# State space products first in each dense block, and the low halves of the dense weights on VectorE

## The chip, the cores and the metric

The kernel runs on one core of a Trainium2 chip. The metric is the time of one execution on the device in microseconds (us). The kernel before takes 3360.59 us, the median of three runs (3353.09 to 3363.12).

## What is computed

A decoder block over 2048 tokens of width 1024: a normalized input is projected to a state space branch (width 512), an attention branch (8 heads of 64, with an indexer that keeps 256 keys for each query) and two sets of gates. The branches are projected back to 1024 columns, gated, added, projected by w_out and added to the input; then follows a gated feed-forward layer (FFN) of width 2816.

```python
h = _rms(x, norm1_g[l])
proj = h @ w_in[l]
u, q, k, v, qi, ki, wi, gates = jnp.split(proj, IN_SPLITS, axis=-1)
y_ssm = _s5_branch(u, ...)
...
y_att = _dsa_branch(q, k, v, qi, ki, wi)
g_ssm, g_att = jnp.split(gates, N_BRANCH, axis=-1)
merged = (jax.nn.sigmoid(g_ssm) * (y_ssm @ w_proj_ssm[l])
          + jax.nn.sigmoid(g_att) * (y_att @ w_proj_attn[l]))
x = x + merged @ w_out[l]
h2 = _rms(x, norm2_g[l])
x = x + (jax.nn.silu(h2 @ w_ffn_gate[l]) * (h2 @ w_ffn_up[l])) @ w_ffn_down[l]
```

## The kernel before

**Precision.** Every large product is made of three matmuls: a float32 operand is split into a high part, rounded to fp32r, and a low part, the rest; high by high, high by low and low by high are summed in PSUM (mm3). Each weight has to be split once: a copy that rounds (hi) and a subtraction (lo).

**Stages.** The input projection, the state space scan and the gates come first. Then three generators run interleaved: state space, attention (for four groups of four tiles of 128 tokens: a search for each query's 256th score, called topk, then the attention of the four tiles), and dense. Dense works in four blocks of 512 tokens; block tb needs the attention of tiles 4tb to 4tb+3. A class (Pace) keeps an estimate of when each engine is free, while the program is recorded, and picks the generator that can go on first; this fixes each engine's order once and for all. At run time every engine goes through its own list in order and waits on semaphores. SP issues all DMAs, in order as well.

**A dense block** (block):
- *Products of the branches.* For each of the 8 column tiles ct (128 columns) and each branch br (0 state space, 1 attention) there are 12 matmuls of 128 x 512 into a PSUM bank f. VectorE multiplies the gate g by it. Gates are stored in DRAM; each branch has two buffers for them, and a buffer is loaded again when its last user is done. Before, the branches alternate after a first group of four, and every second product ends with a merge: the two gated products are added (on POOL or DVE), ScalarE rounds the sum into mg, and DVE or POOL subtracts for its low half.
- *Output projection.* 192 matmuls f<-ww,mg; x1 holds the input rows and the sum.
- *Norm and FFN.* Transposes, then gate and up products (f<-h,ww) and down products (f<-wd,at) added into x1, which is stored to out.

The generator waits before a block until the attention of its four tiles is done (attended). The state space half of a block's input (act, from act_d) and the attention half (act, from att_d) are loaded by load_branch.

**Weights** (Rings, a Loader). In block 0 each item, 512 KB, is loaded to raw (two buffers), split into ww (a ring of four) or wd, and the split pair is stored to DRAM (wc<-ww, 1 MB). Blocks 1 to 3 load the pair again (ww<-wc). Before, an item of the branch products holds one column tile of both branches. hi goes to POOL, DVE or ScalarE and lo to POOL or DVE, whichever the planner has free first (spare); with tight set, DVE is left out of the choice.

**PSUM.** A block has 3 banks in the pool fps, 8 when attention is done for all 16 tiles; during a topk it may borrow 4 more (lend). In the trace nearly every line is L206, since one helper records all operations; names of tiles tell them apart. raw, ww, wd are weights, g gates, mg the merged rows, f the dense PSUM banks; lg, P, pt, th, tl, po, ya belong to attention, and tr, un, cnt, jkd, jka to the search.

Of the kernel before, what the change touches and what calls it, by code (L numbers as in the profile page):

```python
# [12 lines left out]
F32 = mybir.dt.float32  # L13
# [12 lines left out]
KD = D // 128  # L26
# [220 lines left out]
class Loader:  # L247


    def __init__(self, b, pool, bufs, items):  # L250
        self.b, self.pool, self.bufs, self.todo = b, pool, bufs, deque(items)
        self.here, self.count, self.allowed = deque(), 0, 0
        self.fill()
# [8 lines left out]
    def split(self):  # L262
        raw, dest = self.here.popleft()
        self.count += 1
        hi, lo = dest()
        p = self.b.pace
        eng = p.spare(hi, ("POOL", "DVE", "ACT"))
        if eng is p.gpsimd:
            eng.tensor_tensor(hi, raw, self.b.zeros[:, :1].to_broadcast(list(raw.shape)), op=ALU.add)
        elif eng is p.scalar:  # L270
            eng.copy(hi, raw)
        else:
            eng.tensor_copy(hi, raw)
        p.spare(lo).tensor_tensor(lo, raw, hi.bitcast(F32), op=ALU.subtract)
        self.fill()
# [14 lines left out]
class Rings(Loader):  # L290

    def __init__(self, b, pool, bufs, items):
# [70 lines left out]
class Block:  # L366
# [1295 lines left out]
    def weights(self):  # L1662

        a = self.a
        items = []
        for ct in range(KD):
            items.append(("w", lambda raw, ct=ct: [
                (raw[:, i * 512:(i + 1) * 512].rearrange("p (k c) -> p k c", k=4),
                 a[w][0, :, ct * 128:(ct + 1) * 128].rearrange("(k p) c -> p k c", p=128))
                for i, w in enumerate(("w_proj_ssm", "w_proj_attn"))]))  # L1670
        for half in range(2):
# [22 lines left out]

    def block(self, tb, bigp, ld, nps, nd):

# [6 lines left out]
        with ExitStack() as st:  # L1703
            psp = self.pool(st, "fps", nps, PSUM)
            x1 = self.pool(st, "x1", 1).tile([128, nt, D], F32, name="x1")
# [26 lines left out]
            with ExitStack() as sm:  # L1732
                mp = self.pool(sm, "mg", 1)
                mg = mp.tile([128, 2, KD, n], F32R, name="mg")
                with ExitStack() as sp:
# [3 lines left out]
                    def load_gate(ct, br):  # L1739
                        if ct < KD:  # L1740
                            gates[ct, br] = gp.tile([128, n], F32, name=f"g{br}")
                            nc.sync.dma_start(gates[ct, br], self.gate_d[br * KD + ct][hf][:, h0:h0 + n])
# [3 lines left out]
                    act = self.act  # L1746
                    act += [self.load_branch(bigp, br, tb) for br in range(len(act), 2)]
                    self.act = []
                    load_gate(1, 0)
                    load_gate(0, 1)  # L1750
                    load_gate(1, 1)
                    for q, (ct, br) in enumerate([(0, 0), (1, 0), (0, 1), (1, 1)] +
                                                 [(ct, br) for ct in range(2, KD) for br in range(2)]):
                        w = ld.get("w", 1 if q == 1 else 0)
                        w = w.rearrange("p z a (b k c) -> p (z a) b k c", b=2, k=4)[:, :, br]
                        yield ready(w, act[br])
                        ps = bank()
                        for k in range(4):
                            self.mm3(ps, w[:, 0, k], w[:, 1, k], act[br][:, 0, k], act[br][:, 1, k], k == 0, k == 3)
                            ld.tick()  # L1760
                        x = gates[ct, br]
                        nc.vector.scalar_tensor_tensor(x, x, 1.0, ps, op0=ALU.add, op1=ALU.mult)
                        if br == 1:
                            ld.drop("w")
                            x0, x = gates.pop((ct, 0)), gates.pop((ct, 1))
                            spare(x0).tensor_tensor(x0, x0, x, op=ALU.add)
                            self.split(x0, mg[:, 0, ct], mg[:, 1, ct], nc.scalar, spare(x0))
                            load_gate(ct + 2, 0)
                            load_gate(ct + 2, 1)
                        if q == 3:  # L1770
                            self.pace.tight = False
                        if q in (4, 6, 8, 10):
                            t = q // 2 - 2
                            nc.sync.dma_start(x1[:, t], a["x"][0, t0 + t * 128:t0 + (t + 1) * 128])
                fn = self.pool(sm, "fn", 1)
# [85 lines left out]
            ap = self.pool(st, "fa", 5)  # L1861
            tp = self.pool(st, "ft", 2)
            ld.ring("d", self.pool(st, "fd", nd), nd, 2)

# [94 lines left out]
    def run(self):  # L1959
# [12 lines left out]
        def dense(st, gates):  # L1972
# [4 lines left out]
            with ExitStack() as st:  # L1977
# [8 lines left out]
                for tb in range(NB):  # L1986
                    if tb == 1:
                        first.close()
                    yield lambda: self.pace.at("PE") if self.attended >= 4 * (tb + 1) else ("PE", 1e9, None)
                    alone = self.attended == NT  # L1990
                    if alone:
                        self.pace.BIAS = 0.0
                    yield from self.block(tb, bigp, ld, *((8, 2) if alone else (3, 1)))

# [30 lines left out]
```

## Time and profile before

| what | us |
|---|---|
| median of three runs | 3360.59 |
| lowest and highest | 3353.09, 3363.12 |
| the profiled execution | 3357.88 |
| its span | 3355.8 |
| first branch product of block 0 | starts at 980.8 |
| first branch product of block 3 | starts at 2888.7 |

PE is TensorE, PEld its loading of weights, DVE VectorE, ACT ScalarE, POOL GpSimd, SP the queue that issues DMAs. "Busy" counts the time in which an instruction was running. In a timeline row stand the start, the length, engine, line, operation, output <- inputs, and in brackets how long the engine had been idle and what ended that. Matmuls overlap: a row gives some 0.39 us for a 128 x 512 matmul, while they follow each other much faster, so PE's pace is read from how many fit into a stretch.

### The profile page before, as it was taken

How to read it: one execution, taken by the hardware profiler on the slowest of the kernel's cores; microseconds unless marked ns; L12 is line 12 of the kernel's file. 1: busy time of each engine (PE TensorE's matmuls, PEld its weight loads, DVE VectorE, ACT ScalarE, POOL GpSimd, SP SyncE). 2: the span in 40 equal slices, each digit the busy share in tenths (PEclk: the TensorE clock that was granted, in tenths of full speed). 3: DMA queues.
4: the chain of work that ended last, by engine and by line, in shares of the span. 5: the costliest groups of instructions: out<-in, count | busy, mean ns of one | idle time of the engine just before them, and what ended most of it. 6: DMA issues, size and time to landing. Idle time of an engine off the chain costs nothing. (4 is left out here: it accounts for less than half of the span.)

```text
span 3355.8 us, 42712 instructions
## 1 busy us (share of the span) xinstructions
PE 3171.5 (95%) x15528; PEld 2651.1 (79%) x15528; DVE 2106.4 (63%) x4532; ACT 1275.1 (38%) x2211; POOL 638.1 (19%) x628
## 2 busy tenths in 40 slices
PE   7999989899977999989999999999999999999999
PEld 6988767678755788877778888877888888788887
DVE  6555685555587766688687775876886666422223
ACT  3231544445552444346322443665314444210000
POOL 4323676522223311234100000001000000000000
PEclk9999999999988999999999999999999999999999
DMA  5743333534447775656847324366555332755543
GB/s 184 227 122 109 121 89 108 164 120 142 129 166 268 283 257 196 237 182 225 332 187 262 109 93 166 140 236 242 197 213 182 119 108 88 268 195 219 207 177 149
DMA packets 312961, 605.56 MB, mean 180 GB/s; under 512 B 46352, under 2 KB 194608, under 8 KB 282032
## 3 DMA queue, kind: packets, MB, share of 16 engines
q1 hardware_dynamic: 312752, 602.85, 51.7%
q8 instruction: 122, 2.00, 0.2%
q14 instruction: 87, 0.71, 0.1%
HBM read 434.70 MB, written 166.89 MB: 179 GB/s over the span
## 5 line engine op out<-in xcount | busy, mean ns | idle before, releaser
L206 PE MATMUL f<-h,ww 128*128 128x512 f32 (+1 forms) x4416 | 1013.1, 384 | 1.3 <-DVE h L206 0.8
L206 PEld LDWEIGHTS f<-h,ww 128*128 128x128 f32 x4416 | 803.4, 191 | 156.5 <-DVE h L206 1.8
L206 PE MATMUL f<-wd,at 128*128 128x512 f32 x2112 | 518.2, 397 | 28.7 <-DVE t L206 6.5
L206 PEld LDWEIGHTS f<-wd,at 128*128 128x128 f32 x2112 | 396.3, 191 | 116.5 <-DVE t L206 8.1
L206 PE MATMUL gps<-hT,gw 128*128 128x512 f32 x1536 | 387.5, 403 | 4.6 <-ACT gsg L206 3.2
L206 ACT ACTIVATE jka<-S,tr 128x1920 bf16<-128x1920 f32 (+6 forms) x217 | 305.6, 1408 | 180.5 <-DVE tr L206 128.7
L206 PEld LDWEIGHTS gps<-hT,gw 128*128 128x128 f32 x1536 | 288.3, 193 | 68.5 <-ACT gsg L206 5.2
L206 PE MATMUL mm<-w,hT 128*128 128x512 f32 (+1 forms) x1152 | 282.8, 403 | 10.3 <-DVE hT L206 7.2
L206 DVE TENSOR_TENSOR x<-f,x 128x512 f32<-128x512 f32 x352 | 235.1, 686 | 77.0 <-PE f L206 76.4
L206 PEld LDWEIGHTS mm<-w,hT 128*128 128x128 f32 x1152 | 241.5, 239 | 36.7 <-DVE hT L206 8.6
L206 DVE TENSOR_TENSOR tl<-pt,th 128x512 fp32r<-128x512 f32 (+1 forms) x288 | 183.8, 658 | 120.9 <-ACT th L206 119.8
L206 DVE SCALAR_TENSOR_TENSOR t<-t,f 128x512 f32<-128x512 f32 (+1 forms) x123 | 82.1, 668 | 271.8 <-PE f L206 223.6
L206 ACT CAST th<-pt 128x512 fp32r<-128x512 f32 (+1 forms) x288 | 155.5, 563 | 223.8 <-PE pt L206 220.2
L206 PE MATMUL f<-act,ww 128*128 128x512 f32 x768 | 191.8, 411 | 29.5 <-POOL ww L206 20.4
L206 PEld LDWEIGHTS f<-act,ww 128*128 128x128 f32 x768 | 151.2, 199 | 69.5 <-POOL ww L206 24.2
L206 POOL TENSOR_TENSOR g<-g,g 128x512 f32<-128x512 f32 x31 | 39.8, 1285 | 793.9 <-DVE g L206 793.9
L206 PE MATMUL f<-ww,mg 128*128 128x512 f32 x768 | 180.3, 397 | 10.6 <-ACT ww L206 7.0
L206 ACT ACTIVATE P<-P,m 128x1024 f32<-128x1024 f32 (+7 forms) x192 | 172.3, 900 | 46.9 <-DVE m L206 46.8
L206 PE MATMUL lg<-kk,q 128*128 128x512 f32 (+1 forms) x640 | 183.3, 388 | 3.5 <-DMA kk<-kk 3.5
L206 ACT ACTIVATE t<-f 128x512 f32<-128x512 f32 (+1 forms) x92 | 52.9, 575 | 343.8 <-PE f L206 343.7
L206 PEld LDWEIGHTS f<-ww,mg 128*128 128x128 f32 x768 | 147.2, 192 | 43.2 <-ACT ww L206 7.9
L206 ACT CAST at<-t 128x512 fp32r<-128x512 f32 (+1 forms) x92 | 55.2, 600 | 325.4 <-DVE t L206 325.3
(361 smaller groups left out, 4497.9 us busy)
## 6 DMA issues: line engine op xcount, KB each, us to landing
ww<-wc SPq DMA_DIRECT2D x180, 1024.0 KB, 4.9
wd<-wc SPq DMA_DIRECT2D x66, 1024.0 KB, 7.2
wc<-ww SPq DMA_DIRECT2D x60, 1024.0 KB, 7.5
raw<-in_w_in_dram SPq DMA_DIRECT2D x104, 256.0 KB, 3.4
wc<-wd SPq DMA_DIRECT2D x22, 1024.0 KB, 6.3
x<-in_x_dram SPq DMA_DIRECT2D x32, 512.0 KB, 5.3
gate<-gsg SPq DMA_DIRECT2D x64, 256.0 KB, 2.2
g<-gate SPq DMA_DIRECT2D x64, 256.0 KB, 5.7
```

Of the source, the lines that this page charges most:

```text
L206: return f(*args, **kw)
```

## The change

Three things change.

- Items of the branch products hold two column tiles of one branch, state space first. A block makes its eight state space products first, keeps the gated results in x1 (which is free until the input rows are loaded, now after the merge of each pair), and then the eight attention products, each of which ends in a merge. The block starts when the attention of the *block before* is done, and the wait for its own stands between the two halves. The load of the attention half moves there too, or two products ahead of it if attention is done by then.
- The low halves of all dense weights are made by DVE, and the high halves by DVE or ACT, never by POOL. Since only block 0 splits weights, this concerns block 0.
- The pool fps always has 3 banks; when all attention is done, 5 more are lent.

```diff
+    ENGS = ("POOL", "DVE", "ACT")
...
-        eng = p.spare(hi, ("POOL", "DVE", "ACT"))
+        eng = p.spare(hi, self.ENGS)
...
-        p.spare(lo).tensor_tensor(lo, raw, hi.bitcast(F32), op=ALU.subtract)
+        low = p.spare(lo) if "POOL" in self.ENGS else p.vector
+        low.tensor_tensor(lo, raw, hi.bitcast(F32), op=ALU.subtract)
...
+    ENGS = ("DVE", "ACT")
...
-            psp = self.pool(st, "fps", nps, PSUM)
+            psp = self.pool(st, "fps", 3, PSUM)
...
-                    act += [self.load_branch(bigp, br, tb) for br in range(len(act), 2)]
+                    if not act:
+                        act.append(self.load_branch(bigp, 0, tb))
...
+                    kept = x1.rearrange("p t (a c) -> p (t a) c", a=2)
+                    for q in range(2 * KD):
+                        br, ct = q // KD, q % KD
+                        if q == KD:
+                            if self.attended < 4 * (tb + 1):
+                                yield lambda: at("PE") if self.attended >= 4 * (tb + 1) else ("PE", 1e9, None)
+                            if self.attended == NT:
+                                self.pace.BIAS = 0.0
+                                self.spare_banks = 5
+                        if q == KD - 2 or q == KD:
+                            if len(act) == 1 and self.attended >= 4 * (tb + 1):
+                                act.append(self.load_branch(bigp, 1, tb))
+                            if q < KD:
+                                load_gate(0, 1)
+                                load_gate(1, 1)
...
-                        x = gates[ct, br]
-                        nc.vector.scalar_tensor_tensor(x, x, 1.0, ps, op0=ALU.add, op1=ALU.mult)
-                        if br == 1:
+                        x = gates.pop((ct, br))
+                        if br == 0:
+                            nc.vector.scalar_tensor_tensor(kept[:, ct], x, 1.0, ps, op0=ALU.add, op1=ALU.mult)
+                        else:
+                            nc.vector.scalar_tensor_tensor(x, x, 1.0, ps, op0=ALU.add, op1=ALU.mult)
+                            spare(x).tensor_tensor(x, x, kept[:, ct], op=ALU.add)
+                            self.split(x, mg[:, 0, ct], mg[:, 1, ct], nc.scalar, spare(x))
+                        load_gate(ct + 2, br)
+                        if ct % 2 == 1:
                             ld.drop("w")
...
-                    yield lambda: self.pace.at("PE") if self.attended >= 4 * (tb + 1) else ("PE", 1e9, None)
...
+                    if self.attended < 4 * tb:
+                        yield lambda: self.pace.at("PE") if self.attended >= 4 * tb else ("PE", 1e9, None)
+                    yield from self.block(tb, bigp, ld)
```

**Where it moves instructions.** On POOL, at the start of block 0 (ww<-raw,zeros is a high half, ww<-raw,ww a low half, g<-g,g the sum of two gated products), there stands before:

```order
L206 TENSOR_TENSOR ww<-raw,zeros 128x1024
L206 TENSOR_TENSOR ww<-raw,ww 128x1024 x2
L206 TENSOR_TENSOR g_9373<-g_9373,g_9382 128x512
L206 TENSOR_TENSOR mg<-g_9373,mg 128x512
L206 TENSOR_TENSOR ww<-raw,ww 128x1024
L206 TENSOR_TENSOR g_9380<-g_9380,g_9384 128x512
```

In the change only the eight sums of each block are left there. The low halves stand on DVE, among the search's rows; the start of block 0 on DVE in the change:

```order
L206 SCALAR_TENSOR_TENSOR jkd,cnt_7815<-H_8577,tf_7816,jkd 128x320
L206 TENSOR_TENSOR ww<-raw,ww 128x1024
L206 TENSOR_SCALAR un_7812<-cnt_7808 128x1
L206 SCALAR_TENSOR_TENSOR tr_7811<-un_7812,tr_7811 128x1
L206 TENSOR_SCALAR jkd<-H_8577,tf_7816 128x320
```

The 53 low halves that POOL made are now DVE's, and the 24 high halves that POOL made are ACT's and DVE's.

On DVE in block 1, the gated products (g<-g,f before; x<-g,f for the kept ones in the change) and the low halves of the merged rows (mg<-g,mg). Before, from the fifth product on:

```order
L206 SCALAR_TENSOR_TENSOR g_14574<-g_14574,f 128x512
L206 SCALAR_TENSOR_TENSOR g_14576<-g_14576,f 128x512
L206 TENSOR_TENSOR mg<-g_14574,mg 128x512
L206 SCALAR_TENSOR_TENSOR g_14597<-g_14597,f 128x512
L206 SCALAR_TENSOR_TENSOR g_14599<-g_14599,f 128x512
L206 TENSOR_TENSOR mg<-g_14597,mg 128x512
```

And in the change, the last two of the state space half and, after a few rows of the search, the first of the attention half:

```order
L206 SCALAR_TENSOR_TENSOR x_14393<-g_14490,f 128x512
L206 SCALAR_TENSOR_TENSOR x_14393<-g_14506,f 128x512
L206 TENSOR_SCALAR un_13715<-cnt_13711 128x1
L206 SCALAR_TENSOR_TENSOR tr_13714<-un_13715,tr_13714 128x1
L206 TENSOR_SCALAR un_13724<-cnt_13720 128x1
L206 SCALAR_TENSOR_TENSOR tr_13723<-un_13724,tr_13723 128x1
L206 SCALAR_TENSOR_TENSOR g_14510<-g_14510,f 128x512
L206 TENSOR_TENSOR mg<-g_14510,mg 128x512
L206 SCALAR_TENSOR_TENSOR g_14512<-g_14512,f 128x512
L206 TENSOR_TENSOR mg<-g_14512,mg 128x512
```

Before, a merge follows every second product; now none follows the first eight and one follows each of the last eight.

On PE at the start of block 3 (act_24977 and act_24252 are the state space input, act_25469 and act_25605 attention's; po, pt and lg are attention). Before, the end of attention and the first products:

```order
L206 MATMUL f<-wd,at 128x512 x24
L206 MATMUL lg<-ident,s 8x128
L206 MATMUL lg<-r_25427,hsel 128x128 x8
L206 MATMUL f<-act_24977,ww 128x512 x24
L206 MATMUL f<-act_25469,ww 128x512 x24
```

In the change, first the start of the block, then the end of attention:

```order
L206 MATMUL f<-wd,at 128x512 x18
L206 MATMUL po<-th,v 128x256
L206 MATMUL po<-tl,v 128x256
L206 MATMUL f<-act_24252,ww 128x512 x12
L206 MATMUL pt<-ident,P 128x128 x8
L206 MATMUL f<-act_24252,ww 128x512 x12
L206 MATMUL lg<-kk,q 128x512 x4
```

```order
L206 MATMUL lg<-ident,s 8x128
L206 MATMUL lg<-r_25579,hsel 128x128 x8
L206 MATMUL f<-act_25605,ww 128x512 x96
L206 MATMUL f<-ww,mg 128x512 x192
```

Before, attention ended among block 2's last matmuls and two state space products stood between it and the first attention product. Now all eight state space products stand among attention's matmuls, and after the last of them come 48 matmuls lg<-kk,q, 128 transposes pt and 128 matmuls po with no dense matmul between them.

More of the change, by code (lines that the diff above doesn't have):

```diff
@@ L1665, in weights @@
         items = []
[L1666 to L1670, printed above, removed]
+        for w in ("w_proj_ssm", "w_proj_attn"):
+            for c0 in range(0, KD, 2):
+                items.append(("w", lambda raw, w=w, c0=c0: [
+                    (raw[:, i * 512:(i + 1) * 512].rearrange("p (k c) -> p k c", k=4),
+                     a[w][0, :, (c0 + i) * 128:(c0 + i + 1) * 128].rearrange("(k p) c -> p k c", p=128))
+                    for i in range(2)]))
         for half in range(2):
@@ L1693, in load_branch, with block @@
         return z
-    def block(self, tb, bigp, ld, nps, nd):
+    def block(self, tb, bigp, ld):
         nc, a, at = self.nc, self.a, self.pace.at
@@ L1746, in block @@
                     act = self.act
-                    act += [self.load_branch(bigp, br, tb) for br in range(len(act), 2)]
+                    if not act:
+                        act.append(self.load_branch(bigp, 0, tb))
                     self.act = []
                     load_gate(1, 0)
[L1750 to L1755, printed above, removed]
+                    kept = x1.rearrange("p t (a c) -> p (t a) c", a=2)
[13 more added lines that the diff above has]
+                                load_gate(1, 1)
+                        w = ld.get("w")
+                        w = w.rearrange("p z a (b k c) -> p (z a) b k c", b=2, k=4)[:, :, ct % 2]
                         yield ready(w, act[br])
@@ L1760, in block @@
                             ld.tick()
-                        x = gates[ct, br]
-                        nc.vector.scalar_tensor_tensor(x, x, 1.0, ps, op0=ALU.add, op1=ALU.mult)
-                        if br == 1:
-                            ld.drop("w")
[L1765 to L1769, printed above, removed]
+                        x = gates.pop((ct, br))
[7 more added lines that the diff above has]
+                        if ct % 2 == 1:
+                            ld.drop("w")
+                            if br == 1:
+                                t = ct // 2
+                                nc.sync.dma_start(x1[:, t], a["x"][0, t0 + t * 128:t0 + (t + 1) * 128])
                         if q == 3:
                             self.pace.tight = False
-                        if q in (4, 6, 8, 10):
-                            t = q // 2 - 2
-                            nc.sync.dma_start(x1[:, t], a["x"][0, t0 + t * 128:t0 + (t + 1) * 128])
                 fn = self.pool(sm, "fn", 1)
@@ L1862, in block @@
             tp = self.pool(st, "ft", 2)
+            nd = 2 if self.attended == NT else 1
             ld.ring("d", self.pool(st, "fd", nd), nd, 2)
@@ L1988, in dense @@
                         first.close()
-                    yield lambda: self.pace.at("PE") if self.attended >= 4 * (tb + 1) else ("PE", 1e9, None)
[L1990 to L1993, printed above, removed]
+                    if self.attended < 4 * tb:
+                        yield lambda: self.pace.at("PE") if self.attended >= 4 * tb else ("PE", 1e9, None)
+                    yield from self.block(tb, bigp, ld)
         st = ExitStack()
```

## The prediction

> **What bounds the kernel now.** The page comes first, then tables of stretches, then who waited for whom. The first line is the span; the profiled execution took 3357.88 us, so 2.1 us lie around it, and it stands 2.7 us below the median of the three runs shown, inside their spread of 10 us. All sums below are made against 3357.88. The second line gives busy time by engine.
>
> ```profile
> span 3355.8 us, 42712 instructions
> PE 3171.5 (95%) x15528; PEld 2651.1 (79%) x15528; DVE 2106.4 (63%) x4532; ACT 1275.1 (38%) x2211; POOL 638.1 (19%) x628
> ```
>
> PE is busy 95% of the span, so a gain must come out of stretches where PE waits or runs below its pace. The table of stretches gives that pace. Columns: the stretch, its length, busy time with count for PE, PEld, DVE, ACT, POOL, granted clock, DMA share, GB/s.
>
> ```profile
> 971.20:1111.40 140.20, 104.52 (x385) 79.70 (x385) 103.64 (x212) 36.95 (x53) 55.06 (x29) 0.87 0.80 277
> 1400.00:1620.00 220.00, 196.54 (x828) 157.94 (x828) 182.46 (x358) 119.83 (x152) 86.17 (x41) 0.95 0.64 229
> 1620.00:1664.00 44.00, 44.00 (x196) 36.44 (x195) 17.20 (x30) 7.50 (x11) 9.02 (x7) 1.00 0.94 361
> 2246.00:2290.00 44.00, 44.00 (x196) 36.44 (x195) 16.26 (x25) 4.52 (x9) 9.01 (x7) 1.00 0.93 349
> 2884.70:2904.30 19.60, 13.38 (x44) 9.36 (x42) 4.11 (x7) 0.62 (x1) 0.00 (x0) 0.83 0.68 226
> ```
>
> The third and fourth are the branch products of blocks 1 and 2: 196 matmuls in 44.00 us, 0.2245 us each, with nothing lost; but DMA is 0.93 to 0.94 busy there, which matters below. At that pace the 384 matmuls of block 0's products and output projection (first row) need 86.2 us and took 140.2: **54 us lost**. The second row, the end of block 0, has PE idle for 220 - 196.5 = **23.5 us**. The last is the start of block 3: 35 products (7.9 us) and some 1 us for attention's last matmuls in 19.6 us, 10.7 us lost.
>
> In the first stretch two engines end the waits:
>
> ```profile
> PE f L206 <- POOL ww L206: 23.9, 11, 9.5
> PE f L206 <- ACT ww L206: 11.8, 5, 4.6
> ```
>
> Both are the making of weights, 35.7 us. In the second stretch the timeline shows why DVE is late:
>
> ```profile
> 1485.20 2.35 POOL L206 TENSOR_TENSOR ww<-raw,zeros 128x1024 fp32r<-128x1024 f32 x1
> 1485.89 1.67 DVE L206 SCALAR_TENSOR_TENSOR tr<-un,tr 128x1 int32<-128x1 int32 x1
> 1487.62 2.40 POOL L206 TENSOR_TENSOR ww<-raw,ww 128x1024 fp32r<-128x1024 f32 x1
> 1487.66 2.38 DVE L206 SCALAR_TENSOR_TENSOR tr<-un,tr 128x1 int32<-128x1 int32 x1
> 1495.21 0.16 DVE L206 SCALAR_TENSOR_TENSOR tr<-un,tr 128x1 int32<-128x1 int32 x1
> 1497.67 2.92 PE L206 MATMUL f<-wd,at 128*128 128x512 f32 x6 [5.98 <-ACT t L206]
> ```
>
> An update of one number per partition takes 0.16 us alone and 2.38 us while POOL makes weights: DVE ends when POOL ends. PE then stood 5.98 us.
>
> **The change part by part.** First, who makes the weights of block 0:
>
> ```profile
> L206 POOL TENSOR_TENSOR ww<-raw,ww 128x1024 fp32r<-128x1024 f32 x43 | 106.3, 2472 | 153.5 <-ACT ww L206 146.0 <-DVE ww L206 6.3
> L206 POOL TENSOR_TENSOR wd<-raw,wd 128x1024 fp32r<-128x1024 f32 x10 | 25.5, 2550 | 127.0 <-ACT wd L206 126.7
> L206 ACT CAST ww<-raw 128x1024 fp32r<-128x1024 f32 x43 | 44.9, 1047 | 60.1 <-PE f L206 38.7 <-DMA raw<-in_w_out_dram 11.2 <-DMA raw<-in_w_ffn_up_dram 3.6
> L206 DVE TENSOR_TENSOR ww<-raw,ww 128x1024 fp32r<-128x1024 f32 x17 | 20.8, 1225 | 21.7 <-ACT ww L206 21.6
> ```
>
> 53 low parts go from POOL (2.47 to 2.55 us) to DVE (1.225 us): 53 x 1.225 = 65 us more on DVE. Against this stand up to 53 blocked DVE instructions, each of which lost up to 2.2 us; I take DVE's load as unchanged. Each weight is ready 2.47 - 1.225 = 1.25 us sooner.
>
> Stretch 971 to 1111: before, a weight's ACT cast stands behind the merge's cast, which waits for the product before it; with all state space products first, the casts of the attention weights stand ahead of the merges. The waits named above (35.7 us) can go, but 140.2 us at 277 GB/s is 38.8 MB, and at the 361 GB/s of block 1's products that takes 107.6 us. So the gain lies between 0 and 32.6 us. I take **-22**. Stretch 1400 to 1620: between 10 us (two stalls such as the 5.98) and 23.5 us; I take **-20**, as ACT and DVE in a row (1.047 + 1.225) still take 2.3 us where a weight is made just in time. The same blocking stands in block 0's norm, where an instruction of 1.28 us took 3.38 beside POOL and PE stood 4.28:
>
> ```profile
> 1119.57 3.38 DVE L206 SCALAR_TENSOR_TENSOR hh<-x,rr,gB 128x1024 f32<-128x1024 f32 x1 [0.44 <-POOL rr L206]
> 1125.09 1.47 PE L206 MATMUL f<-ident,hh 128*128 128x128 f32 x8 [4.28 <-DVE h L206]
> 2990.59 1.28 DVE L206 SCALAR_TENSOR_TENSOR hh<-x,rr,gB 128x1024 f32<-128x1024 f32 x1
> ```
>
> I take **-3** there, between 0 and 4.3.
>
> Second, gates. The product of a gate and its buffer, in block 2:
>
> ```profile
> L206 DVE SCALAR_TENSOR_TENSOR g<-g,f x16: 679/687/690, 2253.8 to 2291.1; 128x512 f32<-128x512 f32 x16
> L206 POOL TENSOR_TENSOR g<-g,g x8: 1276/1287/1293, 2256.5 to 2291.9; 128x512 f32<-128x512 f32 x8
> L206 ACT CAST mg<-g x8: 620/621/624, 2257.8 to 2293.2; 128x512 fp32r<-128x512 f32 x8
> L206 DVE TENSOR_TENSOR mg<-g,mg x8: 692/693/694, 2258.4 to 2293.9; 128x512 fp32r<-128x512 f32 x8
> DMA to landing us min/median/max: 2.6/5.8/6.7
> g<-gate SPq DMA_DIRECT2D x16, 256.0 KB, 4.5
> ```
>
> (The last row is block 0's, with fewer bytes per us.) Each branch has two gate buffers. Before, branches alternate and all four are in flight, so a buffer returns every fourth product. Now one branch runs alone on its two. In the attention half a buffer is held by 0.687 + 1.287 + 0.621 + 0.693 = 3.29 us of work and then 4.5 to 5.8 us of loading, 8 to 9 us for two products that PE makes in 24 x 0.2245 = 5.39. Only the first two gates are there at the start; three rounds follow. At 4.5 us landing that is 3 x (7.8 - 5.39) = 7 us; at 5.8 it is 11 us, and the first half, where a buffer is held 0.687 us, adds 3 x (6.5 - 5.39) = 3; at the minimum of 2.6, 1.5 us. Three PSUM banks and the projection's first matmuls can hide part. Slower products also leave DMA less crowded, so I take the value by the row of 4.5: **+7 in each of blocks 1, 2 and 3, +21**, bounds 0 and 3 x 14. Block 0's share is inside its -22.
>
> Third, block 3. The wait on attention moves behind the eight state space products, which cover 96 x 0.2245 = 21.6 us. But by the order, dense work now runs ahead of attention everywhere: after the last state space product PE has 32 groups of transposes and value products and 48 score matmuls left with nothing beside them. DVE's work for these, by the end of block 2; then two groups in a row, and the way from att's store to the products:
>
> ```profile
> L206 DVE TENSOR_TENSOR tl<-pt,th 128x512 fp32r<-128x512 f32 x19 | 12.9, 689 | 6.1 <-ACT th L206 5.9
> L206 DVE CUSTOM_DVE_ANT_0 P<-lg,bias,m 128x512 f32<-128x512 f32 x6 | 4.8, 804 | 0.1
> L206 DVE CUSTOM_DVE_ANT_0 P<-lg,bias,rq 128x512 f32<-128x512 f32 x2 | 1.5, 746 | 0.2 <-PE lg L206 0.2
> L206 DVE RECIPROCAL rs<-lg 8x128 f32<-8x128 f32 x1 | 0.9, 935 | 0.0
> L206 DVE TENSOR_TENSOR ya<-po,ot 64x128 f32<-64x128 f32 x6 | 1.7, 280 | 0.8 <-ACT ot L206 0.7
> ...
> 1630.23 1.90 DVE L206 SCALAR_TENSOR_TENSOR g<-g,f 128x512 f32<-128x512 f32 x3 [6.85 <-DMA g<-gate]
> ...
> 2867.12 0.60 PE L206 MATMUL pt<-ident,P 128*128 128x128 f32 x4
> 2868.03 0.60 PE L206 MATMUL pt<-ident,P 128*128 128x128 f32 x4
> ...
> 2890.91 0.38 SPq L206 DMA_DIRECT2D att<-ya  x1
> 2893.90 2.50 SPq L206 DMA_DIRECT2D act<-att  x4
> 2904.28 8.02 PE L206 MATMUL f<-act,ww 128*128 128x512 f32 x27 [0.36 <-DMA act<-att]
> ```
>
> 32 x 0.689 + 18 x 0.804 + 6 x 0.746 + 10 x 0.280 is 44 us, and two scalings (a reciprocal of 0.935 and five shorter rows each) with the reads of accumulators bring some 8: 52 us on DVE. PE needs 32 x 0.91 + 48 x 0.2245 = 40 us. With the part beside the products (about 19 on DVE and 31 on PE) both have some 71 us. I add 7 us for the first gates (6.85 at block 1's start, above), 6 for handing over between engines and 6 for the last scaling, both estimates from the rows' short waits, 3 from att's store to act's load (2890.91 to 2893.90), and 5 until the loaded parts carry the products (10.4 for all four): 98 us for 71 of PE, 27 lost. Before, 10.7 and some 1.5 at attention's last groups: **+15**. Bounds: +2 if only scaling, store and load show, +43 if DVE and PE take turns in the part left alone. Transposes find 3 banks where they had 8: **+2**, 0 to 6.
>
> Sum: -22 - 20 - 3 + 21 + 15 + 2 = **-7**: 3357.88 - 7 = **3351**. The wait before blocks 1 and 2 costs nothing either way, since attention is done before them in both orders.
>
> The stretched DVE row bears on a rule. The Trainium skill, SBUF — State Buffer, section "SBUF: two separate sides", has VectorE and GpSimd contend for one shared pair of ports, as a lock held for a whole instruction. The rows of 2.38 us and 0.16 us agree.
>
> **The rivals.** *Gates hide and weights flow:* with landings of 2.6 to 3.5 us the +21 falls to about 3, or the first two gains reach their bounds (14 us more): some -23, 3335. For it: those minima, and that the new period lowers the GB/s; against it: DMA at 0.93 there. *Attention's end decides (slower):* the stretch from block 2's last dense matmul to attention's products at full pace takes 125 us rather than 98, +27 on the sum: 3378. It makes the kernel slower from 105 us on, measurably from 115. For it: DVE has 52 us where PE has 38, and every step waits for another engine; against it: a group every 0.91 us in the rows above. *The move does nothing:* DVE, already 182 of 220 us busy, makes low parts late behind search rows, and the waits change their name; half the first two gains go (+21): 3372. Against it: the blocked time that leaves DVE. *POOL locked out instead:* DVE's low parts hold up POOL's eight adds in block 0, each by up to 1.225 us, 10 us: 3361. The page named above gives this too, since it counts a VectorE instruction with two SBUF inputs as a holder of the lock; by it the sum would be +3. No row here shows it.
>
> **How the numbers follow.** A measurement of this kernel tells about 0.3%, 10 us, from no change. Forecast 0.42 (0.20 faster, 0.20 within, 0.02 slower, as -7 lies near the edge of 10), own range 3337 to 3366; gates hide 0.25, faster; attention's end 0.17, slower; nothing 0.10 (0.04 within, 0.06 slower); lock 0.06, within. Faster 0.45, same 0.30, slower 0.25. The range runs from 3318, where the gains are near their bounds with half the gates' cost, to 3382, just past attention's end.
>
> **What would show it.** In the changed profile: no POOL row on ww or wd, and tr updates of 0.16 us throughout; 971 to 1111 shortened to about 118 us with DMA above 0.9; PE idle in the end of block 0 down to a few us; DVE waiting for gates in the second halves of blocks 1 to 3, with PE below 44 us per 196 matmuls there; before block 3's attention products some 30 us without dense work in PE. Wrong would be: gates landing in 3 us, a stall over 40 us at block 3, or waits on DVE ww of the old size.

## The result, and the profile after

The changed kernel takes **3395.06 us**, the median of four runs (3390.74 to 3400.80), beside 3357.55 us of the kernel before (four runs on the same chip): a ratio of **1.0112, interval 1.0088 to 1.0136**. 3351 was forecast, with 3318 to 3382 as the range; it is slower, and outside. The profiled execution took 3400.8 us, the longest of the four. One of the four executions of cut_down2, an experiment below, took 11939 us at a granted clock of 0.242 and is left out of its numbers. The head of the changed kernel's page:

```profile
span 3399.0 us, 42684 instructions
PE 3183.7 (94%) x15528; PEld 2659.8 (78%) x15528; DVE 2085.7 (61%) x4589; ACT 1298.5 (38%) x2231; POOL 456.3 (13%) x549
```

The span is 43.2 us longer. PE's busy time grew by 12.2 us with the same 15528 matmuls; the other 31 us are waits. Next, the table of stretches of the changed kernel (columns as in the prediction), first three of the prediction's windows, then cut where its own stages end: the products and output projection of block 1, its FFN, the same two for block 2 with block 3's products at the end of the second, block 3's output projection, and the rest.

```profile
971.20:1111.40 140.20, 101.12 (x383) 78.80 (x384) 86.73 (x209) 35.90 (x50) 11.31 (x10) 0.83 0.77 271
1400.00:1620.00 220.00, 208.07 (x919) 168.81 (x917) 148.31 (x301) 105.82 (x133) 2.52 (x4) 0.97 0.67 238
1620.00:1664.00 44.00, 39.46 (x165) 31.48 (x163) 13.09 (x23) 7.57 (x11) 8.95 (x7) 0.96 0.73 259
...
1606.30:1706.40 100.10, 91.41 (x385) 73.96 (x384) 52.42 (x155) 45.21 (x59) 10.48 (x9) 0.97 0.68 255
1706.40:2251.00 544.60, 525.69 (x2694) 444.11 (x2694) 398.19 (x869) 228.33 (x388) 4.62 (x8) 0.98 0.45 163
2251.00:2345.20 94.20, 88.75 (x385) 72.90 (x383) 50.35 (x130) 45.98 (x49) 10.23 (x8) 0.98 0.68 244
2345.20:2979.40 634.20, 600.81 (x3077) 504.71 (x3076) 431.48 (x909) 242.79 (x398) 9.57 (x9) 0.96 0.43 158
2979.40:3027.40 48.00, 45.56 (x193) 37.20 (x194) 10.81 (x16) 4.16 (x7) 4.94 (x5) 0.96 0.60 227
3027.40:3399.00 371.60, 364.60 (x1665) 303.26 (x1663) 99.08 (x147) 35.05 (x59) 2.07 (x2) 1.00 0.50 186
```

The same stages of the kernel before (the same table):

```profile
1621.90:1709.00 87.10, 87.10 (x385) 71.88 (x383) 53.14 (x131) 22.75 (x32) 10.85 (x9) 1.00 0.74 279
1709.00:2247.30 538.30, 523.28 (x2693) 442.14 (x2693) 394.69 (x872) 253.28 (x408) 4.53 (x7) 0.99 0.45 165
2247.30:2334.40 87.10, 87.10 (x385) 71.89 (x383) 52.88 (x120) 42.00 (x46) 10.84 (x9) 1.00 0.72 268
2334.40:2942.10 607.70, 590.88 (x3078) 498.55 (x3078) 409.29 (x836) 205.94 (x361) 11.61 (x10) 0.98 0.47 168
2942.10:2985.60 43.50, 43.50 (x194) 35.96 (x193) 8.91 (x13) 2.92 (x5) 2.39 (x3) 1.00 0.52 192
2985.60:3355.80 370.20, 364.29 (x1665) 303.18 (x1663) 98.82 (x147) 34.82 (x59) 2.07 (x2) 1.00 0.50 187
```

The prediction's windows first: 971 to 1111 still holds 383 matmuls and its DMA share is 0.77, where some 118 us and above 0.9 were expected; in 1400 to 1620 PE idles 11.9 us rather than 23.5; in 1620 to 1664 there are 165 matmuls rather than 196. That last window now reaches 12 us past the products, into the output projection, and it is there that the matmuls are missing (see *Gates*). Of the stages, each holds the same number of matmuls in both (to within one or two records), so lengths can be subtracted. With the end of block 0's output projection at 1111.7 (before 1111.4) and of block 0 at 1606.3 (before 1621.9):

| stage | forecast | measured |
|---|---|---|
| up to the end of block 0's output projection | -22 | +0.3 |
| rest of block 0 | -23 | -15.9 |
| products and output projection, blocks 1 and 2 | +14 | +13.0 and +7.1 |
| FFN of block 1 | 0 | +6.3 |
| FFN of block 2, products of block 3 | +15 | +26.5 |
| output projection of block 3 (with the gates' delay in its products) | +7 | +4.5 |
| the rest (transposes with three banks) | +2 | +1.4 |
| sum | -7 | +43.2 |

**The first stretch.** PE's waits in 971 to 1111.5, then timeline rows of the same stretch:

```profile
PE f L206 <- DMA act<-att: 13.5, 1, 13.5
PE f L206 <- ACT ww L206: 10.0, 3, 4.9
PE f L206 <- DMA act<-act: 8.7, 1, 8.7
PE f L206 <- DVE ww L206: 8.3, 3, 7.0
```

```profile
1008.36 4.74 SPq L206 DMA_DIRECT2D act<-att  x4
1017.10 24.39 PE L206 MATMUL f<-act,ww 128*128 128x512 f32 x96 [13.54 <-DMA act<-att]
...
1063.46 0.79 PE L206 MATMUL f<-ww,mg 128*128 128x512 f32 x1 [3.18 <-ACT ww L206]
...
1070.03 2.36 DVE L206 TENSOR_TENSOR ww<-raw,ww 128x1024 fp32r<-128x1024 f32 x2
...
1071.30 40.59 PE L206 MATMUL f<-ww,mg 128*128 128x512 f32 x167 [7.05 <-DVE ww L206]
```

The load of the attention half was written into the program at the seventh product, so it left SP at 1008.36, behind weights and gates, and PE stood 13.54 us for it. Later a high half was ready and PE began, but the low half stood on DVE behind search rows until 1070.03, and PE stood another 7.05. The waits on weights have changed their names, and new ones stand beside them.

**Gates.** What DVE waited for in block 1's products and output projection:

```profile
DVE x L206 <- DMA g<-gate: 19.9, 6, 8.6
DVE g L206 <- DMA g<-gate: 5.7, 3, 2.9
```

DVE takes its rows in order: in these 25.6 us (12.0 before) nothing else went on there, the search's rows included. But PE did not lose its time in the products. Timeline rows of PE and SP in the same stage:

```profile
1608.07 43.82 PE L206 MATMUL f<-act,ww 128*128 128x512 f32 x192 [1.61 <-DVE x L206]
...
1647.56 3.73 SPq L206 DMA_DIRECT2D g<-gate  x2
1651.38 0.38 SPq L206 DMA_DIRECT2D ww<-wc  x1
...
1657.31 3.69 SPq L206 DMA_DIRECT2D g<-gate  x2
1659.34 4.58 PE L206 MATMUL f<-ww,mg 128*128 128x512 f32 x12 [4.43 <-DMA ww<-wc]
1661.09 0.39 SPq L206 DMA_DIRECT2D ww<-wc  x1
...
1666.54 39.97 PE L206 MATMUL f<-ww,mg 128*128 128x512 f32 x168 [2.63 <-DMA ww<-wc]
```

The 192 products took 43.8 us, where they had taken 43.7 before. PE stood at the start of the output projection, 4.43 and 2.63 us, for weights. SP issues its loads in order: a gate's load waits there until a merge has freed its buffer, and the weights of the output projection stand behind it. Block 2 shows the same, 43.7 us for its products and one wait of 5.5 us for ww<-wc behind them; block 3 has one of 2.4 us.

**Block 3.** Timeline of PE and SP in the changed kernel, from the first product to the attention half's:

```profile
2842.46 2.91 PE L206 MATMUL f<-act,ww 128*128 128x512 f32 x12
...
2872.23 2.91 PE L206 MATMUL f<-act,ww 128*128 128x512 f32 x12
...
2945.48 0.36 SPq L206 DMA_DIRECT2D att<-ya  x1
2948.01 2.49 SPq L206 DMA_DIRECT2D act<-att  x4
...
2952.44 2.90 PE L206 MATMUL f<-act,ww 128*128 128x512 f32 x6 [9.10 <-issue]
```

From 2842.2 (block 2's end) to the attention products it took 110.2 us. The state space products were used up by 2875, when attention still needed 70 us; PE had no dense matmul for 77 us, where the prediction had some 30. Before, attention's last store stood at 2890.9, block 3's start at 2888.7. So attention was late by 54.6 us and dense work early by 46, and the question is why.

Dense matmuls done (the table of stretches, of the tile f alone; the second and third numbers are PE's busy time with its count) between 971 and the last store of attention's second group, before and in the change:

```profile
971.00:1386.70 415.70, 306.42 (x1256) 234.02 (x1257) 58.19 (x88) 11.71 (x21) 0.95 0.71 248
```

```profile
971.00:1437.20 466.20, 350.62 (x1461) 272.07 (x1462) 69.90 (x105) 13.50 (x24) 0.94 0.71 252
```

The second group ended 50.5 us later, and PE had by then made 205 more dense matmuls, which at 0.2245 us is 46 us. Attention was late because PE's list has more dense work ahead of it.

### The profile page after: what moved, and what is told of

Read it like the earlier page. It is cut to its first block, busy times and chain, and to the rows that moved or that the text cites. A ratio compares the mean times of both kernels' runs of the same rounds, so it can differ in the third digit from the quotient of the medians.

```text
span 3399.0 us, 42684 instructions
## 1 busy us (share of the span) xinstructions
PE 3183.7 (94%) x15528; PEld 2659.8 (78%) x15528; DVE 2085.7 (61%) x4589; ACT 1298.5 (38%) x2231; POOL 456.3 (13%) x549
## 5 line engine op out<-in xcount | busy, mean ns | idle before, releaser
L206 ACT ACTIVATE jka<-S,tr 128x1536 bf16<-128x1536 f32 (+6 forms) x217 | 305.6, 1408 | 201.1 <-DVE tr L206 105.8
L206 PE MATMUL f<-ww,mg 128*128 128x512 f32 x768 | 190.8, 411 | 33.8 <-DMA ww<-wc 14.9
L206 POOL TENSOR_TENSOR g<-g,x 128x512 f32<-128x512 f32 x32 | 40.9, 1277 | 942.7 <-DVE g L206 756.0
```

Of the source, the lines that this page charges most:

```text
L206: return f(*args, **kw)
```

## The experiments

Ratios are to the kernel before, measured beside each on the same chip; times are medians. First one part of the change at a time, and two remedies.

**order_only**: the change, but weights made as before.

```diff
 class Rings(Loader):
-    ENGS = ("DVE", "ACT")
```

> The change without its part on the low halves: POOL, VectorE and ScalarE make weights as before. Theory 1 (the low halves on VectorE hold up the search and attention, so that attention comes about 50 us late to its end): the last att<-ya returns from 2945.5 us to about 2890, the stretch from block 2's last dense matmul to the end of block 3's products shrinks from 137 to 60 to 70 us, the end of block 0 loses its 15.6 us again; time 3375 to 3385. Theory 2 (the order alone makes attention late, since dense work runs ahead): the last att<-ya stays near 2945, the stretch near 135, and with the end of block 0 lost the time is 3405 to 3415. In both the products and output projection of blocks 1 and 2 keep their 100 and 94 us.

3391.78 us, ratio 1.0095 [1.0080, 1.0110]. Attention's last store came at 2926.8, block 2 ended at 2905.6. The stretch from block 2's output projection to the end of block 3's products took 608.3 us (2355.2 to 2963.5; before 607.7, in the change 634.2). So the loss of 26.5 us there is gone, as theory 1 has it; but the order alone costs 30 us elsewhere, in block 0 (8 us from its first product to its end) and in the products and output projections of blocks 1 to 3. Attention came 36 us late, not at 2890, and the time lies between the forecasts of the two theories.

**lows_only**: the kernel before with the low halves on DVE.

```diff
+    ENGS = ("POOL", "DVE", "ACT")
...
-        eng = p.spare(hi, ("POOL", "DVE", "ACT"))
+        eng = p.spare(hi, self.ENGS)
...
-        p.spare(lo).tensor_tensor(lo, raw, hi.bitcast(F32), op=ALU.subtract)
+        low = p.spare(lo) if "POOL" in self.ENGS else p.vector
+        low.tensor_tensor(lo, raw, hi.bitcast(F32), op=ALU.subtract)
...
+    ENGS = ("DVE", "ACT")
```

The second ENGS is that of Rings, the class of the dense weights.

> The kernel before with nothing but the low halves on VectorE (high halves on VectorE or ScalarE). Theory 1: the end of block 0 gains some 15 us, but attention ends 40 to 55 us later than its 2890.9, and block 3 waits for it with nothing to do: the loss is 25 to 45 us there, the time 3365 to 3385. Theory 2: attention ends where it did, the gain of block 0 stays, the time is 3335 to 3345. In both the products of blocks 1 and 2 with their output projection take 87 us each, as before.

3367.53 us, 1.0027 [1.0017, 1.0037]. Block 0 ends at 1597.0, 24.9 us earlier than before. But the second group ends at 1429.6, 43 us late, and block 2 is over at 2803.5 while the last store comes at 2902.5. PE in the stretch between (table of stretches):

```profile
2803.50:2900.30 96.80, 79.56 (x463) 65.08 (x461) 66.76 (x146) 50.47 (x93) 0.00 (x0) 0.92 0.06 18
```

Attention is alone for 96.8 us, and PE idles 17.2 of them. Theory 1 holds: what block 0 gains is given back before block 3.

**gates4**: the change with one ring of four gate buffers, in place of two for each branch; the first four gates are loaded ahead of the products.

```diff
-                    gp = self.pool(sp, "mgate", 2)
+                    gp = self.pool(sp, "mgate", 4)
...
-                        load_gate(ct + 2, br)
+                        load_gate(q + 4)
```

> The change with the four gate buffers as one ring of four, loaded four products ahead, in place of two for each branch; same memory. If the buffers' round trip is what lengthens the branch products, the products and output projection of blocks 1, 2 and 3 lose 13, 7 and 4 us again (back to 87, 87 and 44 us) and the time falls by 20 to 25 us to 3370 to 3375. If DMA has no room for gates and weights at once (its share was 0.68 in both stretches), the waits move to the weights and the gain is under 8 us.

3367.27 us, 1.0022 [1.0012, 1.0032]: **28 us less** than the change. Block 1's products and output projection, block 2's, and the long stretch to the end of block 3's products:

```profile
1603.00:1692.00 89.00, 89.00 (x384) 73.08 (x384) 56.36 (x165) 47.87 (x61) 10.31 (x8) 0.98 0.75 278
2239.90:2327.80 87.90, 87.39 (x385) 71.81 (x383) 54.15 (x148) 50.92 (x53) 10.30 (x8) 1.00 0.72 261
2327.80:2956.20 628.40, 595.52 (x3078) 500.75 (x3078) 421.89 (x868) 224.06 (x381) 10.90 (x10) 0.96 0.44 160
```

Back from 100.1 to 89.0 and from 94.2 to 87.9, with the DMA share up: the round trip of two buffers was the cause, not DMA's room, as the first forecast had it. PE's waits on ww<-wc went from 7.1 us to none in block 1 and from 5.5 to 0.5 in block 2. Block 0's first stretch fell as well (its output projection ends at 1103.1), so part of that stretch's lost gain was gates too. The last row keeps 20.7 of its 26.5 us.

**early_att**: the change, the attention half loaded before the third product.

```diff
-                        if q == KD - 2 or q == KD:
+                        if q in (2, KD):
                             if len(act) == 1 and self.attended >= 4 * (tb + 1):
                                 act.append(self.load_branch(bigp, 1, tb))
+                        if q == KD - 2:
```

> The change with the load of block 0's attention half issued four products earlier (before the third state space product rather than the seventh). If this load, standing late in SP's queue, is what ate the gain of the first stretch, the wait of 13.5 us before the first attention product goes, the stretch 971 to 1111.7 ends 8 to 13 us earlier, and the time falls to 3382 to 3388. If the weights take its place (low halves behind search rows on VectorE, or raw behind the 2 MB of the load), the stretch keeps 135 to 141 us and the time stays within 5 us of 3395.

3393.93 us, 1.0103 [1.0088, 1.0118], no gain that can be told from nothing. The first attention product came 13.2 us earlier (1003.9), but the stretch ended only 4.4 us earlier, at 1107.3. PE's waits in it:

```profile
PE f L206 <- ACT ww L206: 17.5, 3, 10.3
PE f L206 <- DVE ww L206: 9.7, 7, 5.2
PE f L206 <- ACT jka L206: 9.2, 1, 9.2
```

The wait for the load is gone and weights took its place (27.2 us on ww, where the change had 18.3), as the second expectation said.

The next four ask whether dense work or attention sets the end.

**ring_pool, ring_early, ring_pool_early**: gates4 with order_only's line; gates4 with early_att's line; both.

> The order of the change with the ring of four gate buffers, but weights made by POOL, VectorE and ScalarE as before. Theory 3 (attention's own chain of search and attention sets when block 3's second half may start, and the low halves and the gate waits on VectorE lengthen it; the time is the last att<-ya plus some 445 us): the last att<-ya comes at 2890 to 2905 instead of 2923 with the ring alone, and the time is 3338 to 3352, below both kernels. Rival (dense work is the bound): the 10 to 15 us at the end of block 0 that the low halves on VectorE had gained are lost, and the time is 3375 to 3385, above the 3367 of the ring alone.

> The change with the ring of four gate buffers and block 0's attention half loaded four products earlier. Theory 3: dense work gets some 10 us further ahead, attention hardly moves; 3362 to 3369, within 5 us of the ring alone (3367). Rival (dense work is the bound): the 10 us show in full, 3354 to 3358.

> Both of the two others: weights made as before, the ring of four, the attention half of block 0 loaded four products earlier. Theory 3: within 5 us of the run without the earlier load, 3335 to 3352. Rival (dense work is the bound): 8 to 12 us below that run.

3367.66 (1.0038 [1.0027, 1.0048]), 3365.18 (1.0031 [1.0017, 1.0044]) and 3367.59 us (1.0038 [1.0024, 1.0051]). The earlier load is worth nothing in either; but it made the first stretch only 1.6 us shorter in ring_early and 1.6 us longer in ring_pool_early, so these two runs do not tell the theories apart. ring_pool missed both its forecasts of the time: attention's last store came at 2905.7, block 2 ended at 2891.1, and the time is that of gates4. Two of its stages, the first stretch and the one from block 2's output projection to the end of block 3's products:

```profile
971.00:1094.80 123.80, 96.65 (x386) 76.41 (x387) 99.77 (x205) 33.13 (x47) 45.53 (x23) 0.86 0.85 301
...
2337.20:2944.90 607.70, 590.22 (x3077) 497.47 (x3077) 401.26 (x811) 197.78 (x355) 10.91 (x10) 0.98 0.46 165
```

The first is 16.6 us shorter than before, of all runs the nearest to the forecast of 22; the second is as long as before. With the ring, weights shared with POOL and low halves on DVE throughout come out equal: what the one loses by the end of block 0 (it ends at 1616.9; gates4 1601.0) the other loses before block 3 (628.4 us against 607.7).

**cut_down2**: the change with a third of block 2's down products left out.

```diff
+                            if tb == 2:
+                                nc.tensor.matmul(p, acts[f][:, 0, tl], w[:, 0, f, cl], start=f == 0, stop=False)
+                                nc.tensor.matmul(p, acts[f][:, 1, tl], w[:, 0, f, cl], start=False, stop=f == 1)
+                                continue
```

> The change with one of the three matmuls left out in every down product of block 2 (176 matmuls, 39.5 us of PE at 0.2245 us; block 2's rows of the output lose the part low weight by high input). Theory 3: dense work reaches block 3 about 35 us earlier and waits that much longer for attention, whose last store moves by less than 10 us; 3385 to 3395 against 3395 of the change. Rival (dense work is the bound): the time falls by 35 to 40 us, to 3355 to 3360.

3378.44 us, 1.0068 [1.0044, 1.0091]: some 17 of the 39.5 us. Block 3's first product came 47 us earlier (2795.4), attention's last store 17.7 us earlier (2927.8), and the span is 17.6 us shorter. Outside both expectations, nearer to theory 3: the time follows attention's last store, but attention does get part of the PE time freed. That it gets no more because of its own steps on VectorE and ScalarE is likely, not shown.

So neither chain alone is the bound; both must arrive together. How PE's list divides PE's time is then what counts. The number of dense matmuls that stand in the list ahead of the end of attention's groups 2, 3 and 4, and the measured last store of each group:

| kernel | ahead of groups 2, 3, 4 | last stores | time |
|---|---|---|---|
| before | 1238, 3538, 6144 | 1386.7, 2084.5, 2890.9 | 3357.6 |
| the change | 1442, 3778, 6240 | 1437.2, 2140.6, 2945.5 | 3395.1 |
| order_only | 1286, 3538, 6180 | 1406.8, 2096.9, 2926.8 | 3391.8 |
| lows_only | 1442, 3796, 6144 | 1429.6, 2125.3, 2902.5 | 3367.5 |
| gates4 | 1442, 3682, 6240 | 1431.3, 2108.6, 2923.0 | 3367.3 |

At groups 2 and 3 the counts nearly foretell the lateness of the change (204 matmuls or 45.8 us, measured 50.5; 240 or 53.9, measured 56.1). At the last they give 96 or 21.6 us of 54.6: what PE has lost in waits by then does not stand in the list.

The three kernels with low halves on DVE from the start have 1442 ahead of group 2. The planner counts some 1.15 us of DVE for each low half (1024 elements at its 1.05 ns, and 0.07), so attention's rows look late to it, and it puts dense ones ahead. The last four experiments move this.

**late_before** and **late_ring**: lows_only and gates4, but low halves go to DVE only when attention's second group is done. The edit of late_ring against the change, without the lines of the ring:

```diff
+        late = self.b.attended >= 8
-        eng = p.spare(hi, self.ENGS)
+        eng = p.spare(hi, ("DVE", "ACT") if late else ("POOL", "DVE", "ACT"))
...
-        low = p.spare(lo) if "POOL" in self.ENGS else p.vector
+        low = p.vector if late else p.spare(lo)
```

> The kernel before, with the low halves on VectorE (high ones on VectorE or ScalarE) only from the end of attention's second group on; until then POOL is in the choice as before. PE's list then has 1238 dense matmuls ahead of the end of the second group as before (1442 in the change and with low halves on VectorE throughout) and 6144 ahead of the last. Theory 4 (the run follows PE's list: attention is late by as many dense matmuls as stand ahead of it, and PE's losses add up wherever neither generator covers them): the second group ends at 1385 to 1390, the end of block 0 gains 10 to 20 us, and these are kept, since at the end dense and attention are as balanced as before: 3340 to 3350. Rival (block 3 waits for attention in any case, so what dense gains it waits longer): 3355 to 3362.

> The order of the change with the ring of four gate buffers, and low halves on VectorE only from the end of attention's second group on. PE's list has 1238, 3538 and 6156 dense matmuls ahead of the ends of the three later groups, as with weights made by POOL. Theory 4: the time of that kernel (3367.7) less the 10 to 15 us at the end of block 0: 3350 to 3358. Rival (attention's end decides): within 5 us of 3367.

late_before: 3355.34 us, 0.9992 [0.9983, 1.0002]. The second group ends at 1386.6, as before, and block 0 at 1601.6, 20.3 us earlier; but block 2 is over at 2845.6 and block 3 waits until 2883.8. The rival was right: the wait takes the gain back. **late_ring: 3345.64 us, 0.9969 [0.9958, 0.9980]**, faster than both kernels and better than either expectation. Its long stretch to the end of block 3's products, and the start of block 3 up to the first attention product:

```profile
2320.60:2928.60 608.00, 587.03 (x3078) 495.25 (x3078) 401.84 (x815) 197.85 (x354) 10.76 (x10) 0.98 0.46 165
...
2874.40:2903.70 29.30, 23.30 (x105) 18.83 (x104) 7.30 (x11) 0.62 (x1) 0.00 (x0) 0.98 0.86 286
```

634.2 became 608.0 us; late_before has 619.2. Attention's last store came at 2888.9, and PE was busy for 23.3 of the 29.3 us before the first attention product, nearly all of it with state space products: this is what the order was able to give, 9.7 us against late_before, once gates and attention were not late. Against ring_pool the gain lies in the rest of block 0, 501.5 us where that has 522.1.

**free_before** and **free_ring**: lows_only and gates4, but the planner's clock of DVE is set back after each low half, so that it counts no time for them: the same instructions in another order.

```diff
+        t = p.free["DVE"]
         low.tensor_tensor(lo, raw, hi.bitcast(F32), op=ALU.subtract)
+        if low is p.vector:
+            p.free["DVE"] = t
```

> The kernel before with all low halves on VectorE, but the planner counts no time of VectorE for them, so that it places attention's rows earlier: 950, 3100 and 5754 dense matmuls ahead of the ends of the later groups (before: 1238, 3538, 6144). The same instructions as with low halves on VectorE alone, in another order. Theory 4: attention's last store comes 60 us or more before 2890, block 3 waits for nothing, and the time falls to 3325 to 3345. Rival (VectorE has no time for the low halves beside attention, whatever the order): PE waits in block 0 for VectorE's products of attention, 30 us or more, and the time is 3365 to 3400.

> The change with the ring of four gate buffers, and the planner counts no time of VectorE for low halves: 974, 3100 and 5754 dense matmuls ahead of the ends of the later groups (with the ring alone: 1442, 3682, 6240). Theory 4: no stretch without dense work before block 3's attention products; 3330 to 3345. Rival (VectorE has no time for the low halves beside attention): 3370 to 3400.

3379.77 us, 1.0074 [1.0058, 1.0090], and 3383.75, 1.0083 [1.0068, 1.0098]. That the order follows the planner's count and the run follows the order holds: against the kernel before, free_before has 288 fewer matmuls ahead of the second group (64.7 us), and that group ended 62.9 us earlier (1323.8), the last 65.3 us earlier; block 3 waited for nothing (2919.3 straight after block 2). Against lows_only, which has the same instructions, it is 492 fewer (110.5 us) and 105.8 us earlier: so it is the order, and not the time that DVE spends on low halves, that makes attention late. But the gain failed to come, and the time is that of the rival, though not from its place: PE did not stand at attention's products, but at the end of block 0 and the start of block 1, long after the second group's end, where weights were late. DVE was busy there for 221.5 of the 249.4 us from 1400 to block 1. PE's waits of free_before from 1400 to 1700:

```profile
PE f L206 <- DVE wd L206: 18.4, 6, 6.4
PE f L206 <- DVE x L206: 12.7, 4, 9.4
```

So attention too far ahead (3379.8) is no better than attention too far behind (lows_only, 3367.5).

## Why the prediction was wrong

The profile lies 50.2 us above the sum: 22.3 of them in the first stretch, 11.5 in the stage that ends with block 3's products, 7.1 in the rest of block 0, 6.3 in block 1's FFN, 6.1 in the products and output projections of blocks 1 and 2, less 3.1 in what follows.

**The step that failed first: "The waits named above (35.7 us) can go ... I take -22"** for the stretch 971 to 1111. It gave +0.3. The waits on POOL did go, but the step took DMA's speed as the only other limit. It left out what block 0's gates cost, which it counted as inside the -22, and low halves that stand on DVE behind search rows (8.3 us of PE's waits). From 971 to the end of the output projection it takes 140.7 us in the change, 132.1 with the ring of gates (gates4), 138.7 with weights shared with POOL (order_only) and 123.8 with both (ring_pool); before, 140.4. The late load of the attention half (13.5 us) was a wait too, but taking it away was worth 4.4 us at most (early_att): one wait removed there gives place to the next. This is the prediction's own rival "the move does nothing", which it gave a chance of 0.10; the rival names the low halves, but not the gates.

**The step that failed second: "Third, block 3 ... 98 us for 71 of PE, 27 lost"**, and with it the term +15. It took 110.2 us, of which PE was busy 89.4, and +26.5 in that stage. The rival "attention's end decides" has the right wait; its 105 us, the point from which the whole kernel is slower, rested on gains that did not come. (It sets DVE's 52 us against 38 of PE, where the prediction's own sum has 40; nothing hangs on that.) The sentence "by the order, dense work now runs ahead of attention everywhere" was right, but its price was worked out for the last stretch alone, and its cause was sought in the new order. order_only and lows_only show it apart: without the low halves on DVE the stage takes 608.3 us (+0.6), with them and the old order 635.9 (2317.4 to 2953.3, +28.2). The low halves made attention late in block 0, through the planner's list, and block 3 paid. So the +15 was the price of something that the order alone does not cost.

**"I take DVE's load as unchanged"** was right for DVE (2106.4 us busy before, 2085.7 after) and missed that the planner does not see the blocking it removes, only the 1.15 us it adds.

**End of block 0, -20:** -15.9 with the norm's -3 in it; right in kind. Updates of tr, between 971 and 1620, before and after (minimum, median, maximum in ns):

```profile
L206 DVE SCALAR_TENSOR_TENSOR tr<-un,tr x75: 158/160/2383, 972.1 to 1618.2; 128x1 int32<-128x1 int32 x60, 128x2 int32<-128x2 int32 x15
```

```profile
L206 DVE SCALAR_TENSOR_TENSOR tr<-un,tr x44: 159/160/163, 977.0 to 1606.7; 128x1 int32<-128x1 int32 x36, 128x2 int32<-128x2 int32 x8
```

The counts differ since the search of the third group starts some 50 us later in the change. The norm's instruction fell from 3.38 to 1.28 us, but the wait behind it only from 4.28 to 3.44, as two low halves (2.35 us) now stand behind it on DVE; so -3 was some -1.

**Gates, +21:** the right cause, near the right size, by a wrong path. The prediction priced slower branch products, two of them in 7.8 us where PE needs 5.39. They ran at full pace in blocks 1 and 2 (43.8 and 43.7 us for 192). What the round trip made late were the weights of the output projection, behind the gates in SP's queue, a step that the sum did not have, so that 24.6 us (13.0, 7.1 and 4.5) came near 21 by luck. Why DVE's delay did not reach the products is not shown; PSUM banks that a block may borrow are the likely cover. The ring takes 21.9 of the 24.6 us away (100.1 to 89.0, 94.2 to 87.9, 48.0 to 43.5), and 28 us from the whole.

**"The wait before blocks 1 and 2 costs nothing"** held: attention's second group was done at 1437.2, before block 1 (1606.3), and its third at 2140.6, before block 2 (2251.0). **"POOL locked out"** did not decide: POOL's eight adds of block 0 took 1.26 to 1.29 us each, as ever.

**Open:** the FFN of block 1, 6.3 us longer (9.6 in gates4, 3.5 in late_ring, 2.9 in ring_pool, 0.2 in order_only). No one part of the change explains these: PE waited 6.2 us for loads of wd there in the change and 0.9 in gates4, which lost more. And the rest of block 0 (to its end, from the end of its output projection) is 11.6 us longer in ring_pool than before, 522.1 against 510.5, which takes most of its 16.6 us back; why is open.

## What to carry to other kernels

Where two chains share an engine whose order is fixed beforehand, count how much of the one stands ahead of milestones of the other, before and after: here 204 matmuls at one milestone foretold 46 of 50 us of lateness, though 96 at the last foretold only 22 of 55. A gain in one chain is worth nothing at their meeting point until the other arrives earlier as well, so a stall taken out early and an order that covers a wait were each worth little alone and 0.3% together. When a new order leaves only two of four buffers in flight, size the ring for the time of the round trip, and look at what is queued behind the instruction that waits: here it was not the products that use the gates, but the weights behind them in SP's queue.

## What had not been expected of the hardware

The blocking of DVE by POOL also goes the other way. In the changed kernel one low half on DVE met a select on POOL, which takes 0.29 us otherwise (timeline):

```profile
1488.05 1.22 DVE L206 TENSOR_TENSOR wd<-raw,wd 128x1024 fp32r<-128x1024 f32 x1
1488.21 1.22 POOL L206 TENSOR_SCALAR_AFFINE_SELECT S<-S 128x128 f32<-128x128 f32 x1 [20.87 <-DVE S L206]
...
1501.06 0.29 POOL L206 TENSOR_SCALAR_AFFINE_SELECT S<-S 128x128 f32<-128x128 f32 x1 [11.63 <-DVE S L206]
```

It ended 0.16 us after the low half. The Trainium skill, SBUF — State Buffer, section "SBUF: two separate sides", has the shared pair held for the whole instruction by whichever comes first, a VectorE instruction with two SBUF inputs among them; this row agrees. It cost 0.9 us here; two later selects, of 0.71 and 0.84 us, also ended 0.15 us after a DVE instruction that was running when they started.

Where PE waited, more was lost than its idle time. In block 1's products and output projection PE idled 8.7 us, and its 385 matmuls took 91.4 us of busy time, where they had taken 87.1 without a wait, at a granted clock of 0.97 against 1.00: 13.0 us for 8.7 of waiting. The output projection, where the waits stand, has the low clock: 0.94 from 1651.9 to 1706.4, against 1.00 from 1608 to 1651.9. In the long stretch before block 3's output projection it was 16.6 us more idle and 9.9 us more busy time.
